# A two-layer trunk on one core: x of a token group asked for ahead of its weights, two small loads moved behind

## The chip, the cores and the metric

The kernel runs on one core of a Trainium2 chip. The metric is the device time of one execution in microseconds (us). The core has five engines with a queue of instructions each: PE (matrix products), DVE and POOL (elementwise), ACT (functions and copies) and SP, which here only issues transfers. An engine takes its instructions in the order of its queue; where one waits for a semaphore, all behind it wait too. Transfers between memory and the core run on 16 DMA engines.

## The reference, cut to what matters

The kernel computes a trunk of two layers for two batches with the same weights, 512 and 2048 tokens, width 1024:

```
def _even_layer(x, ...):
    p = _rmsnorm(x, norm_w) @ w_in                    # 1024 -> 4224 columns
    shifted = _centred_shift(p[..., :EVEN_SHIFT], mu_prev, mu_next)
    r, k, v, w_lat, a_lat = _split(shifted, ...)
    y_a = _rwkv7(...)                                 # w_up, a_up: rank 64 -> 512, two directions
    y_b = _dilated_attention(...)
    return x + concat(y_a * silu(gate_a), y_b * silu(gate_b)) @ w_out
def _odd_layer(x, ...):                               # gated linear attention, two directions
    ...
```

A final normalization by rows ends it. What this change touches is the first line (x is normalized and multiplied by `w_in`) and the loading of `w_up` and `a_up`, the up projections of the recurrent branch.

## The kernel before, in words

The 2560 tokens are worked in five groups of 512. For one group, `dense` multiplies the normalized, transposed x with blocks of 128 columns of the weights. All factors are split into a high and a low part, so that a block is 24 products of 128x128 by 128x512 (three for each of eight slices of the depth): `pd<-xh,wh`, `pd<-xl,wh`, `pd<-xh,wl` at L296.

`xprep` makes x ready: it loads four tiles of 128 tokens (L234), squares each on ACT (L237), finds the root of the mean on DVE (L239 and L205 to L210), scales the tiles by pairs on DVE (L242), transposes them on PE (`pt<-cst,x`, L248), multiplies by the norm's weights on ACT (L249) and splits them (L250, L251). The transposes of one slice take parts of all four tiles, so that the first block product needs all of x.

`weights` loads a block's weights in halves (`w`, L265, four buffers) and splits them into `wh` (L273) and `wl` (L274). `dense` creates it and takes the first two splits before it asks for x.

`open_prep` opens the buffers of the recurrent branch's preparation and loads at once the up projections (`PT<-in_wup`, L368, two loads of 512 KB), splits them (`wup`, cast on ACT L369, subtraction on DVE L370), and loads the pattern of the scan (`scan`, L372). The source of these two loads is 64 rows, broadcast to twice 64. They are read by `prep` (L455, L466), which runs beside the second group.

Further on, `inverts` inverts small triangular matrices for the recurrence: DVE makes `LD` (L580), PE multiplies (`pt<-LD,LO`, L589). `recurrence` then runs 80 steps (`pg`, `pc`), with attention beside it; out projections (`po`) and the second layer follow. `mix` and `weave` set how much of a side work is written between the steps of a main one, but the order of the instructions in the engines' queues is set by a scheduler when the program is built: it follows its own estimate of times, so that a small change at the start can move instructions anywhere behind it.

Of the kernel before, what the change touches and what calls it, by code (L numbers as in the profile page):

```python
# [117 lines left out]
class Trunk:  # L118
# [159 lines left out]
    def dense(self, parts, xT=None):  # L278

        nc = self.nc  # L280
        flat = [(p, n, *job) for p, (_, jobs) in enumerate(parts) for n, job in enumerate(jobs)]
        ws = self.weights(flat)
        split = [next(ws), next(ws)]
        xT = [] if xT is None else xT
        for p, n, _, m, sink in flat:
            if n == 0 and parts[p][0]:
                yield from parts[p][0](xT)
            ps = self.pd.tile([128, 512], F32, name="pd")
            byk = n == 0 or n == len(parts[p][1]) - 1
            for half in range(2):  # L290
                wh, wl = split.pop(0)
                split.extend(w for w in (next(ws, None),) if w)
                three = [((wh, k, hi), (wh, k, lo), (wl, k, hi)) for k, (hi, lo) in enumerate(xT[4 * half:4 * half + 4])]
                three = [e for t in three for e in t[:3 if byk else 2]] + [t[2] for t in three if not byk]
                for j, (a, k, x) in enumerate(three):
                    nc.tensor.matmul(ps[:m], a[:, k, :m], x, start=half == 0 and j == 0, stop=half == 1 and j == 11)  # L296
                    if j % 6 == 5:
                        yield 1280
            sink(ps)
# [62 lines left out]
    def open_prep(self, es):  # L362
        self.pq = self.pool(es, "pq", 1)
        self.ps_p = self.pool(es, "psp", 3, space=PSUM)
        self.wup = [self.pq.tile([128, 2, 512], F32R, name=f"wup{n}") for n in range(2)]
        for n, w in enumerate(self.wup):
            raw = self.pq.tile([128, 2048], F32, name="PT", bufs=2)[:, 0:1024].rearrange("p (z c) -> p z c", z=2)
            self.nc.sync.dma_start(raw, self.I["wup"][64 * n:64 * n + 64][None].to_broadcast([2, 64, 2, 512]))  # L368
            self.nc.scalar.copy(w, raw)  # L369
            self.nc.vector.tensor_tensor(w[64:128], raw[64:128], w[64:128].bitcast(F32), op=OP.subtract)  # L370
        self.scan = self.pq.tile([128, 520], F32, name="scan")
        self.nc.sync.dma_start(self.scan, self.I["scan"])  # L372
# [775 lines left out]
    def gla_unit(self, z, h, t0, first, S, tens, late):  # L1148
# [12 lines left out]
        for n in (0, 2):  # L1161
            duo = order[n:n + 2]
            At, kx = (gp.tile([128, 2, 128], F32, name=n, bufs=3) for n in ("at", "kx"))
            nc.gpsimd.memset(At[b, :, a], 0.0)
            pa = self.pa.tile([128, 2, 256], F32, name="pa")
            for i, s in enumerate(duo):
                kc = whole(K, s)
                kl = kc[:, 64:192] if z == 0 else kc[:, 0:128]
                nc.tensor.matmul(pa[:, i, b], kl, Q[:, s, 2 * se], start=True, stop=True)  # L1169
            for i, s in enumerate(duo):  # L1170
                nc.tensor.transpose(pa[:, i, 128:256], whole(KX, s), self.cc("ident"))
            for i, s in enumerate(duo):
                nc.tensor.matmul(pa[a, i, a], K[:, s, 2 * fi], Q[:, s, 2 * fi], start=True, stop=True)  # L1173
                within[s] = At[:, i], kx[:, i]
            nc.scalar.copy(kx, pa[:, :, 128:256])
            for c in (a, b):
                V.tensor_tensor(At[c, :, c], pa[c, :, c], m[c, None, :].to_broadcast([64, 2, 64]), op=OP.mult)
            nc.scalar.copy(At[a, :, b], pa[a, :, b])
            yield 860
        for s in order:  # L1180
            At, kx = within[s]
            po = self.pgo.tile([128, 2, 256], F32, name="pgo")
            qc = whole(Q, s)
            ql = qc[:, 0:128] if z == 0 else qc[:, 64:192]
            nc.tensor.matmul(po[:, 1], kx, Vt[:, s], start=True, stop=True)  # L1185
            nc.tensor.matmul(po[:, 0], At, Vt[:, s], start=True, stop=False)  # L1186
            nc.tensor.matmul(po[:, 0], ql, S, start=False, stop=True)  # L1187
            V.scalar_tensor_tensor(S, S, d[:, s, 2:3], po[:, 1], op0=OP.mult, op1=OP.add)
            if not late:
                nc.scalar.copy(o[:, s], po[:, 0])  # L1190
            else:
                V.tensor_tensor(o[:, s], po[:, 0], o[:, s], op=OP.add)
            yield 1300
# [67 lines left out]
    def whole(self):  # L1261
        I = self.I
        shifted, rest = [12] + list(range(12)), list(range(13, 33))
        left, right, base = ExitStack(), ExitStack(), ExitStack()

        def on(side, es):

            es.close()
            self.side = side
            return es  # L1270

        self.open_inv(on("right", base))
        self.open_prep(on("left", left))
        self.open_dense(on("right", right), 0)
        xT = []

        def part(t, blocks):

            xT.clear()
            return self.dense([(lambda x: self.xeven(x, t), self.even(t, blocks))], xT)  # L1280

        def behind(t):

            yield from self.inverts()
            yield from self.prep(1, t)

        self.run(part(0, shifted))
        self.mix(part(512, shifted), self.prep(0, 0), 0.6)
        for t in (1024, 1536, 2048):
            self.mix(part(t, shifted + rest), behind(t - 512), 0.72)  # L1290
        self.mix(part(0, rest), self.weave(self.inverts(), self.prep(1, 2048), 0.8), 1.0)
        self.open_dense(on("right", right), 2)
        xT.clear()
        self.run(self.xeven(xT, 512))
        self.xes.close()

        def beside():
            inv = self.inverts()
            for n in self.dense([(None, self.even(512, rest))], xT):
                yield n  # L1300
                next(inv, None)
            yield from inv
            right.close()
            base.close()
            for seq in range(2):
                self.open_att(on("right", right), seq)
                yield from self.attention(seq)

        self.open_rec(on("left", left))
        self.mix(self.recurrence(), beside(), 1.3)  # L1310
        self.open_out(on("right", right), 0, I["woe"])
        for t in (0, 1024, 1536, 512):
            self.run(self.out0(t))
        self.open_dense(on("left", left), 1)
        xT = []
        self.run(self.odd(1024)[0](xT), self.out0(2048))
        self.open_gla(on("right", right))
        until = lambda g, t: self.run(iter(lambda: next(g), t))
        g0, g1 = self.gla(0, PARTS[1:], (2048,), self.states()), self.gla(1, PARTS[:0:-1], (512, 1024, 1536), self.states())
        for t, now in ((1024, ()), (512, ((g0, 512), (g0, 1024))), (2048, ((g1, 2048),)), (1536, ((g0, 1536), (g1, 1536)))):  # L1320
            self.run(self.dense([(None, self.odd(t)[1])], xT) if t == 1024 else self.dense([self.odd(t)]))
            for g in now:
                until(*g)
        self.run(x for xs in zip(iter(lambda: next(g0), 2048), iter(lambda: next(g1), 1024)) for x in xs)
        self.run(self.dense([self.odd(0)]))
        self.run(g0)
        self.open_out(on("left", left), 1, I["woo"])
        self.fn = self.op.tile([128, 1024], F32, name="fn", bufs=1)
        f = I["fn"]
        self.nc.sync.dma_start(self.fn, bass.AP(tensor=f.tensor, offset=f.offset, ap=[[0, 128], [1, 1024]]))  # L1330
        S = self.states()
        p = chain(self.gla(0, [0], (), S), self.gla(1, [0], (0,), S))
        self.run(x for xs in zip(g1, p) for x in xs)
        self.run(g1, p, *(self.out1(t) for t in (1536, 2048, 1024, 512, 0)))
        right.close()
        left.close()
# [25 lines left out]
```

## Time and profile before

| what | value |
|---|---|
| median of 3 runs | 4209.18 us |
| the three runs | 4193.99, 4209.18, 4211.28 us |
| the profiled execution | 4192.46 us, its span 4190.7 us |
| PE busy | 3809.9 us (91% of the span) |
| DVE busy | 2624.2 us (63%) |
| ACT, POOL busy | 1790.0, 1465.4 us |
| mean granted clock of PE | 0.933 |

Busy times are sums over the span; what an engine's idle time costs depends on who waits for it there. A row of the order of time gives the start, the length, the engine, the line, and the tile written and read; in square brackets it says how long the engine stood idle before, and what ended that. "SPq" is the queue from which SP issues transfers.

### The profile page before, as it was taken

How to read it: one execution, taken by the hardware profiler on the slowest of the kernel's cores; microseconds unless marked ns; L12 is line 12 of the kernel's file. 1: busy time of each engine (PE TensorE's matmuls, PEld its weight loads, DVE VectorE, ACT ScalarE, POOL GpSimd, SP SyncE). 2: the span in 40 equal slices, each digit the busy share in tenths (PEclk: the TensorE clock that was granted, in tenths of full speed). 3: DMA queues.
4: the chain of work that ended last, by engine and by line, in shares of the span. 5: the costliest groups of instructions: out<-in, count | busy, mean ns of one | idle time of the engine just before them, and what ended most of it. 6: DMA issues, size and time to landing. Idle time of an engine off the chain costs nothing. (4 is left out here: it accounts for less than half of the span.)

```text
span 4190.7 us, 76827 instructions
## 1 busy us (share of the span) xinstructions
PE 3809.9 (91%) x28720; PEld 3001.9 (72%) x28720; DVE 2624.2 (63%) x6104; ACT 1790.0 (43%) x3685; POOL 1465.4 (35%) x1431
## 2 busy tenths in 40 slices
PE   5998988898787898999999997999999999988997
PEld 4776767677566776677777675778788787867776
DVE  4788887877978646456676755332354526576775
ACT  3453534443343234444544443112354526464552
POOL 2554635445554323112222322222343424232321
PEclk9999999999889888898998988999999999989999
DMA  5554645555445444534454435654554454555553
GB/s 161 186 190 141 191 139 180 163 174 166 149 149 165 131 126 139 161 110 148 127 157 120 138 85 175 207 176 138 161 166 155 156 159 156 180 191 171 172 177 126
DMA packets 516360, 655.78 MB, mean 156 GB/s; under 512 B 48083, under 2 KB 340179, under 8 KB 514963
## 3 DMA queue, kind: packets, MB, share of 16 engines
q1 hardware_dynamic: 422899, 562.72, 43.1%
q10 hardware_dynamic: 80464, 72.09, 5.4%
q0 software_dynamic: 12624, 16.06, 1.5%
q8 instruction: 227, 3.72, 0.4%
q14 instruction: 146, 1.20, 0.1%
HBM read 444.57 MB, written 206.36 MB: 155 GB/s over the span
## 5 line engine op out<-in xcount | busy, mean ns | idle before, releaser
L296 PE MATMUL pd<-xh,wh 128*128 128x512 f32 (+1 forms) x2320 | 944.2, 410 | 48.7 <-DVE wh L273 24.2
L296 PE MATMUL pd<-xl,wh 128*128 128x512 f32 (+1 forms) x2320 | 944.5, 407 | 20.3 <-POOL xl L251 19.7
L296 PE MATMUL pd<-xh,wl 128*128 128x512 f32 (+1 forms) x2320 | 690.4, 404 | 16.8 <-DVE wl L274 15.0
L274 POOL TENSOR_TENSOR wl<-w,wh 128x512 fp32r<-128x512 f32 (+1 forms) x290 | 396.3, 1367 | 670.6 <-PE pd L296 365.3
L296 PEld LDWEIGHTS pd<-xh,wh 128*128 128x128 f32 (+1 forms) x2320 | 447.1, 193 | 163.2 <-DVE wh L273 31.2
L296 PEld LDWEIGHTS pd<-xl,wh 128*128 128x128 f32 (+1 forms) x2320 | 448.3, 193 | 125.1 <-POOL xl L251 26.3
L296 PEld LDWEIGHTS pd<-xh,wl 128*128 128x128 f32 (+1 forms) x2320 | 439.7, 192 | 119.5 <-DVE wl L274 20.4
L273 DVE CAST wh<-w 128x512 fp32r<-128x512 f32 (+1 forms) x290 | 171.5, 591 | 346.6 <-PE pd L296 293.8
L273 ACT CAST wh<-w 128x512 fp32r<-128x512 f32 (+1 forms) x290 | 177.6, 613 | 327.8 <-PE pd L296 201.7
L896 ACT ACTIVATE P<-P,O 128x128 f32<-128x128 f32 (+2 forms) x480 | 198.1, 450 | 229.9 <-DVE O L894 222.6
L1031 PE MATMUL po<-oh,yh 128*128 128x512 f32 x640 | 257.4, 403 | 40.6 <-ACT yh L1020 40.6
L885 PE MATMUL pS<-Ks,Qs 64*128 64x256 f32 x896 | 274.2, 587 | 6.3 <-DVE O L894 4.1
L274 DVE TENSOR_TENSOR wl<-w,wh 128x512 fp32r<-128x512 f32 (+1 forms) x290 | 239.7, 827 | 62.8 <-PE pd L296 56.3
L1031 PE MATMUL po<-ol,yh 128*128 128x512 f32 x640 | 255.9, 401 | 0.0
L894 DVE CUSTOM_DVE_ANT_0 P<-pS,msk 128x128 f32<-128x128 f32 (+2 forms) x480 | 153.8, 353 | 156.9 <-PE pS L885 102.0
L1031 PE MATMUL po<-oh,yl 128*128 128x512 f32 x640 | 248.4, 400 | 2.6 <-DVE yl L1021 2.4
L934 PE MATMUL pV<-Vt,Pt 128*64 128x65 f32 (+1 forms) x3072 | 182.0, 246 | 20.4 <-DVE O L935 7.5
L934 PEld LDWEIGHTS pV<-Vt,Pt 128*64 128x64 f32 (+1 forms) x3072 | 136.8, 148 | 78.0 <-issue 23.6
L723 POOL TENSOR_TENSOR X<-X,wcs 64x512 f32<-64x512 f32 x76 | 80.1, 1054 | 319.5 <-PE pc L761 181.5
L885 PEld LDWEIGHTS pS<-Ks,Qs 64*128 64x128 f32 x896 | 150.3, 270 | 54.6 <-issue 16.8
L1018 POOL TENSOR_TENSOR yr<-yr,yg 128x1024 f32<-128x1024 f32 x40 | 97.8, 2446 | 257.3 <-DMA yr<-d_yT 170.9
L546 POOL TENSOR_TENSOR PTr<-PTr,wc 128x512 f32<-128x512 f32 x80 | 84.9, 1061 | 285.4 <-PE pg L536 261.0
(285 smaller groups left out, 7612.2 us busy)
## 6 DMA issues: line engine op xcount, KB each, us to landing
w<-in_we SPq DMA_DIRECT2D x330, 256.0 KB
w<-in_wi SPq DMA_DIRECT2D x240, 256.0 KB
d_f<-PT SPq DMA_DIRECT2D x40, 1024.0 KB
PTr<-d_f SPq DMA_DIRECT2D x77, 512.0 KB
d_sg<-st SPq DMA_DIRECT2D x80, 256.0 KB
yr<-d_yT SPq DMA_DIRECT2D x40, 512.0 KB
yg<-d_sg SPq DMA_DIRECT2D x40, 512.0 KB
Vg<-d_gv SPq DMA_DIRECT2D x40, 512.0 KB
```

The source lines that it names most:

```text
L273: (nc.vector.tensor_copy, nc.scalar.copy)[h](wh[:, :, :m], w[:, :, :m])
L274: (nc.vector, nc.gpsimd)[h].tensor_tensor(wl[:, :, :m], w[:, :, :m], wh[:, :, :m].bitcast(F32), op=OP.subtract)
L296: nc.tensor.matmul(ps[:m], a[:, k, :m], x, start=half == 0 and j == 0, stop=half == 1 and j == 11)
L546: nc.gpsimd.tensor_tensor(bk, bk, self.wc[:, z, c, :, None].to_broadcast([128, 4, 128]), op=OP.mult)
L723: nc.gpsimd.tensor_tensor(nx, x[lo, 0], self.wcs[:, z, c, :, None].to_broadcast([64, 8, 64]), op=OP.mult)
L885: nc.tensor.matmul(o2, a[o], b[o], start=True, stop=True)
L894: V.tensor_tensor_reduce(P[:, h, :nk], pss[h][:, u, off:off + nk], mask, 1.0, 3e38, op0=OP.add, op1=OP.min, accum_out=m)
L896: nc.scalar.activation(P[:, h, :nk], P[:, h, :nk], AF.Exp, scale=-1.0, bias=m)
L934: nc.tensor.matmul(po[q, h, :], Pt[:r, i, h, q], v[:r, h, :], start=i == 0, stop=i == n - 1)
L1018: nc.gpsimd.tensor_tensor(y, y, g, op=OP.mult)
L1031: nc.tensor.matmul(ps[u][e], a[:, k], b[:, k, c], start=k == 0 and j == 0, stop=k == 7 and j == 2)
```

## The change

Two edits. In `dense`, the first two steps of the first part's `xprep` (which issue the loads of x, square and scale it) are now written before `weights` is created, and the rest of it where all of it stood. In `open_prep`, only the buffers are opened; the loads of the up projections and of the scan's pattern are in a function of its own, `load_prep`, which is called after 14 steps of the first group's `dense` (two steps of x, eight slices, one block of four steps).

```
         flat = [(p, n, *job) for p, (_, jobs) in enumerate(parts) for n, job in enumerate(jobs)]
+        xT = [] if xT is None else xT
+        fill = parts[0][0](xT) if parts[0][0] else iter(())
+        for _ in range(2):
+            yield from (n for n in (next(fill, None),) if n)
         ws = self.weights(flat)
         split = [next(ws), next(ws)]
-        xT = [] if xT is None else xT
         for p, n, _, m, sink in flat:
-            if n == 0 and parts[p][0]:
-                yield from parts[p][0](xT)
+            if n == 0:
+                yield from parts[p][0](xT) if p else fill
...
     def open_prep(self, es):
         self.pq = self.pool(es, "pq", 1)
         self.ps_p = self.pool(es, "psp", 3, space=PSUM)
+
+    def load_prep(self):
         self.wup = [self.pq.tile([128, 2, 512], F32R, name=f"wup{n}") for n in range(2)]
...
-        self.run(part(0, shifted))
+        first = part(0, shifted)
+        for _ in range(14):
+            next(first)
+        self.load_prep()
+        self.run(first)
```

What the scheduler makes of it. The queue of SP at the start of the program, before (`w` are weights, `x` the tokens, `PT<-in_wup` the up projections):

```order
L154 DMA cst<-in_cst 128x579
L157 DMA par<-in_par 128x88
L368 DMA PT<-in_wup 128x1x1024 x2
L372 DMA scan<-in_scan 128x520
L265 DMA w<-in_we 128x512 x4
L234 DMA x<-in_xp 128x1024 x4
L356 DMA rope<-in_rope 128x2x512
L265 DMA w<-in_we 128x512 x3
```

The same place now:

```order
L154 DMA cst<-in_cst 128x579
L157 DMA par<-in_par 128x88
L234 DMA x<-in_xp 128x1024 x4
L265 DMA w<-in_we 128x512 x4
L373 DMA PT<-in_wup 128x1x1024 x2
L377 DMA scan<-in_scan 128x520
L359 DMA rope<-in_rope 128x2x512
L265 DMA w<-in_we 128x512 x3
```

x and the first four weight tiles went to the front, the up projections and the scan's pattern behind them.

The queue of ACT at the start, as a piece of the difference (+ is now; `wup` are the up projections, `xr<-pt` is the first step on the transposed x):

```order
-L369 CAST wup_110<-PT 128x1024
-L369 CAST wup_111<-PT 128x1024
-L273 CAST wh<-w 128x512
+L1367 UNCONDITIONAL_BRANCH
+L237 ACT_TABLE_LOAD
 L237 ACTIVATE xr,ss<-x 128x1024 x4
+L273 CAST wh<-w 128x512
+L374 CAST wup_330<-PT 128x1024
+L374 CAST wup_331<-PT 128x1024
 L249 ACTIVATE xr<-pt,par 128x512 x2
```

The casts of the up projections moved behind the four squares of x, and stand ahead of L249. On DVE, before, the two subtractions of `wup` stand ahead of all of x's steps; now they stand between the scaling of the first pair of x and that of the second:

```order
L242 TENSOR_SCALAR x<-x,xry 128x1024 x2
L205 TENSOR_SCALAR xri<-ms 128x2
L273 CAST wh<-w 128x512
L206 TENSOR_SCALAR xry<-xri 128x2
L274 TENSOR_TENSOR wl<-w,wh 128x512
L208 SCALAR_TENSOR_TENSOR xru<-xry 128x2
L209 TENSOR_TENSOR xru<-xru,ms 128x2
L210 SCALAR_TENSOR_TENSOR xry<-xru,xry 128x2
L208 SCALAR_TENSOR_TENSOR xru<-xry 128x2
L209 TENSOR_TENSOR xru<-xru,ms 128x2
L375 TENSOR_TENSOR wup_330<-PT,wup_330 64x1024
L210 SCALAR_TENSOR_TENSOR xry<-xru,xry 128x2
```

The second subtraction follows two rows later, and after two more small steps the scaling of the second pair (L242). So both stand ahead of it.

Further on, on PE, where the last inversions are multiplied (`pt<-LD,LO`) between the block products of a group and the first steps of the recurrence, before:

```order
L296 MATMUL pd<-xh_12278,wl 128x512
L296 MATMUL pd<-xh_12280,wl 128x512
L296 MATMUL pd<-xh_12282,wl 128x512
L296 MATMUL pd<-xh_12284,wl 128x512
L536 MATMUL pg<-PTr 128x128 x8
L747 MATMUL pc<-X,BK 64x64 x8
L550 MATMUL pc<-cst,PTr 128x128 x2
L589 MATMUL pt<-LD,LO 32x32 x64
```

And now:

```order
L299 MATMUL pd<-xh_12276,wh 128x512
L299 MATMUL pd<-xl_12277,wh 128x512
L299 MATMUL pd<-xh_12270,wl 128x512
L299 MATMUL pd<-xh_12272,wl 128x512
L299 MATMUL pd<-xh_12274,wl 128x512
L299 MATMUL pd<-xh_12276,wl 128x512
L541 MATMUL pg<-PTr 128x128 x2
L594 MATMUL pt<-LD,LO 32x32 x64
L762 MATMUL pc<-X,RS 64x64 x8
```

Counted by the block products (`pd`) that stand ahead of it in the program, this multiplication moved back by 60, and the one after it by 42.

## Rows read from the trace of the kernel before

**Rows 1.** The page: span, and busy us (share) by engine.

```profile
span 4190.7 us, 76827 instructions
PE 3809.9 (91%) x28720; PEld 3001.9 (72%) x28720; DVE 2624.2 (63%) x6104; ACT 1790.0 (43%) x3685; POOL 1465.4 (35%) x1431
```

**Rows 2.** Busy time of each engine in stretches of the span.

```profile
core 0: us, PE busy (x) PEld busy (x) DVE busy (x) ACT busy (x) POOL busy (x), PEclk, DMA share, GB/s
0.00:47.00 47.00, 4.29 (x16) 2.75 (x17) 13.21 (x41) 10.35 (x15) 3.10 (x15) 1.00 0.44 136
47.00:140.00 93.00, 91.28 (x429) 74.58 (x428) 52.69 (x92) 42.16 (x71) 43.96 (x42) 1.00 0.50 162
...
1060.00:1400.00 340.00, 274.04 (x2153) 215.78 (x2149) 297.14 (x452) 126.22 (x244) 173.12 (x162) 0.88 0.47 144
1400.00:2500.00 1100.00, 1038.00 (x12691) 775.60 (x12691) 643.67 (x2329) 514.47 (x1318) 267.85 (x283) 0.90 0.46 134
```

**Rows 3.** PE's waits, whole span: for whom, total us, times, longest us.

```profile
PE pt L248 <- DVE x L242: 42.1, 2, 39.7
```

**Rows 4.** The start in order of time, SP's queue: start us, us.

```profile
1.21 0.42 SPq L157 DMA_DIRECT2D par<-in_par  x1
1.66 1.32 SPq L368 DMA_DIRECT2D PT<-in_wup  x2
3.03 9.85 SPq L372 DMA_DIRECT2D scan<-in_scan  x1
12.92 4.67 SPq L265 DMA_DIRECT2D w<-in_we  x4
17.64 12.87 SPq L234 DMA_DIRECT2D x<-in_xp  x4
```

**Rows 5.** The start in order of time, DVE, ACT and PE.

```profile
3.72 0.17 DVE L162 TENSOR_SCALAR c<-par 128x13 f32<-128x13 f32 x1 [3.72 <-DMA par<-in_par]
...
17.31 1.04 ACT L369 CAST wup<-PT 128x1024 fp32r<-128x1024 f32 x1 [15.27 <-DMA PT<-in_wup]
...
29.53 1.04 ACT L369 CAST wup<-PT 128x1024 fp32r<-128x1024 f32 x1 [11.17 <-DMA PT<-in_wup]
30.60 1.22 DVE L370 TENSOR_TENSOR wup<-PT,wup 64x1024 fp32r<-64x1024 f32 x1 [10.99 <-ACT wup L369]
...
34.08 1.06 ACT L237 ACTIVATE xr<-x 128x1024 bf16<-128x1024 f32 x1 [1.97 <-DMA x<-in_xp]
...
40.26 0.16 DVE L239 TENSOR_SCALAR ms<-ss 128x2 f32<-128x2 f32 x1
...
42.62 1.42 DVE L242 TENSOR_SCALAR x<-x,xry 128x1024 f32<-128x1024 f32 x2
...
47.03 1.20 PE L296 MATMUL pd<-xh,wh 128*128 128x512 f32 x2
...
54.36 0.97 DVE L273 CAST wh<-w 128x512 fp32r<-128x512 f32 x1 [0.69 <-PE pd L296]
```

**Rows 6.** DMA queues from 7 to 13 us: packets, MB, share of 16 engines.

```profile
DMA packets 79, 0.32 MB, mean 53 GB/s; under 512 B 2, under 2 KB 2, under 8 KB 79
...
q1 hardware_dynamic: 77, 0.32, 12.8%
```

**Rows 7.** Busy times from 32 to 36 us, columns as in rows 2.

```profile
32.00:36.00 4.00, 0.00 (x0) 0.00 (x0) 3.00 (x4) 1.89 (x4) 1.26 (x1) 1.00 0.92 342
```

**Rows 8.** Who reads wup: durations ns, first and last start us.

```profile
L455 PEld LDWEIGHTS pp<-lat0h,wup x40: 186/190/331, 130.2 to 1272.7; 128*128 128x128 f32 x40
```

**Rows 9.** PE's waits from 1060 to 1400 us.

```profile
PE pt L589 <- DVE LD L580: 10.2, 2, 6.9
```

**Rows 10.** PE in order of time near 1400 us.

```profile
1394.04 3.83 PE L589 MATMUL pt<-LD,LO 32*32 32x32 f32 x128 [6.91 <-DVE LD L580]
...
1403.35 0.40 PE L296 MATMUL pd<-xh,wh 128*128 128x512 f32 x1
1403.59 0.40 PE L296 MATMUL pd<-xl,wh 128*128 128x512 f32 x1
```

## The prediction, made before the changed kernel ran

> **What bounds the kernel now.** I read the page's busy times first: the matrix engine (PE) works 3809.9 us of a 4190.7 us span, DVE 2624.2 [rows 1]. So time can only be won where PE stands idle, 381 us in all. The table of stretches shows where: 42.7 us before 47 us, then 1.7 us of the 93 to 140, 66 us of the 340 between 1060 and 1400 (there DVE is busy 297), 62 us of the 1100 after it [rows 2]. The table of PE's waits names the ends: 42.1 us in two waits for the scaled x (DVE, L242), one of them 39.7 us long [rows 3]. That is the very start. Everything else that ends on x is 2.4 us. So of the edit in `dense`, which holds for every token group, only the first group has a wait to give back. The order says the same: of the later groups the x loads stand behind the same number of weight loads as before, but for one tile of the 512 group (two weight loads later).
>
> Then I read the start in order of time. SP asks for cst, par, the two up-projection loads (PT<-in_wup), scan, four weight tiles, and only then x; the issue of scan is held for 9.85 us, that of x for 12.87 us [rows 4]. ACT gets the first up-projection tile at 17.31, the second at 29.53, the first x at 34.08; the second x pair is scaled from 42.62, and the first block product starts at 47.03 [rows 5]. Why so late, with 16 DMA engines? From 7 to 13 us only the up-projection loads move: 77 packets, 0.32 MB, 12.8% of 16 engines, so two engines at 26 GB/s each [rows 6]. Later, with x and w in the queue, 342 GB/s pass [rows 7].
>
> The Trainium skill ("DMA: Bandwidth & Descriptors", section "Why a DMA increments its semaphore by 16 and not by 1") has the rule: a transfer is spread over the largest number of engines up to 16 that divides the slowest dimension, always the lowest-numbered ones; the up-projection's source begins with a dimension of 2 (the broadcast), so 2 engines, the same two for both loads. The trace agrees with the same two: were they two pairs, rows 6 would have to read 25%. By the other reading the second load would land some 10 us sooner and the gain below would be 13 us in place of 3.
>
> **The change, part by part.**
>
> *x and w in front on SP.* x (4 x 512 KB) and w (4 x 256 KB) now stand ahead of the two up-projection loads. par, issued at 1.21, is used at 3.72 [rows 4, 5], so data follow an issue by about 2.5 us, and x, issued from about 1.7, moves from about 4.2. One sixteenth of x is 131 kB, at 26 GB/s 5.0 us: x has landed by some 11 us, against 34.
>
> *But the two up-projection loads still stand in front of the first block product.* The order on ACT and DVE (shown in the section on the change) decides: ACT has both casts of wup ahead of the first activation on the transposed x (L249), and DVE has both subtractions ahead of the scaling of the second x pair (L242). An engine's instructions go in order, so x waits for the second up-projection load after all. That load now stands behind x and w on its two engines: one sixteenth of 3.15 MB is 197 kB, 7.5 us at 26 GB/s, 9.2 us at 342 GB/s over all engines. It was cast at 29.53; I add 7.5: 37.0. From there: the cast until the subtraction, 30.60 - 29.53 = 1.07; the subtraction 1.22; two small steps, 0.4; from the start of L242 to the first block product 47.03 - 42.62 = 4.41 [rows 5]. Sum 37.0 + 7.1 = 44.1 us. **Start: -2.9 us.** Bounds: if the two engines lose nothing on the way (2 x 512 KB over two engines at 26 GB/s is 20.2 us, from 4.2 + 7.5), the load is there at 31.9 and the start gains 8; by 9.2 us it gains 1.2; if each of the two loads begins moving only 2.5 us after the one before has ended, it loses 3.8. I take 2.9, since it rests on the landing that was seen.
>
> *Weights of the third block, scan and rope.* They now stand behind the up-projection on those two engines: 260, 512 and 256 KB, a sixteenth each, is 2.5 us after about 37, so about 40 to 42. The third block's first weight tile was cast at 54.36 [rows 5]; the cover is some 10 us, cost nothing. wup is first read by prep at 130.2 [rows 8], the scan's pattern in the step after: nothing. The rest of the edit (two steps of x ahead of the weight casts) adds no instruction.
>
> *The order further on.* The scheduler lays the whole program out again. Up to about 850 us, and from 2500 to 3700, PE's order is nearly the same; between, blocks of it move. The largest move with a wait behind it: the last inversion's products (pt<-LD) come 60 and 42 block products later. Before, PE stood 6.91 us at 1394.04 until DVE had LD [rows 10]. DVE has LD at nearly the same place of its own order, so the block products now fill that wait. After it PE is busy 1038 of 1100 us [rows 2], so what it did early it needn't do late. Ends: a gain of 10.2 us (both waits for LD in that stretch [rows 9], one of 6.9 and one of 3.3), a loss of 14 (below). I take the row itself: **-6.9 us.**
>
> Sum: -2.9 - 6.9 = -9.8 us. Against the profiled execution, 4192.46 us (span 4190.7), that is 4182.7; the median of the three runs, 4209.18, lies 16.7 above it, and on that scale the forecast is 4199.4 us.
>
> **Rivals.**
>
> *A. x reaches PE without the up-projection.* If wup's casts did not hold ACT and DVE, the last x at about 11 would be followed by one square (1.06), the twelve small DVE steps (42.62 - 40.26 = 2.36) and the 4.41 to the first product [rows 5]: 19; with the weights' casts in between some 20, a gain of 27; with the 6.9 above, 4175. For it: x does land that early. Against it: the order of two engines.
>
> *B. Slower: the recurrence gets its inverse later.* Place: 1394 us, where the last inversions end. They stand 60 block products later on PE, at 0.235 us a product (the starts in [rows 10]) 14.1 us. The recurrence reads these inverses through memory. If the recurrence, and not PE, bounds the stretch to 2500, the 14.1 us are lost and the 6.9 not won: 4209.2 - 2.9 + 14.1 = 4220.4. It decides as soon as the recurrence waits for its inverse. For it: 1060 to 1400 is bound by DVE (297 of 340). Against it: PE is 94% busy behind it.
>
> *C. The change does not do what it says.* The start stays at 47 us or later (bound +3.8), the order moves nothing net: 4206 to 4213.
>
> **How the numbers follow.** Forecast 0.50, A 0.06, B 0.16, C 0.28. The three runs of before lie 17 us apart, as much as all cases but A differ; a change of under 0.5% (21 us) can't be told from none here. Faster than that is below 4188: A nearly whole (0.05), and from the forecast and C what the scatter gives (0.19): 0.24. Slower is above 4230: a third of B and a little of C, 0.07. The rest, 0.69, is no change. The range reaches from A's upper part to B's time: 4174 to 4220; the forecast's own is 4186 to 4211.
>
> **What would show it.** In the profile after: x loads issued from about 1.7 us; the first x square at 7 to 9 us, not 34; the second cast of wup at about 37 (32 to 39), ACT idle before it and waiting for that DMA; the first block product at about 44. If that product starts before 30, A is right; at 47 or later, C. Near 1390 no wait of PE for LD of several us: the forecast; a wait of the recurrence for its inverse or PE idle between 1400 and 1500: B. The sum is wrong if some other stretch between 850 and 2500 moves by more than 10 us.

## The result

The changed kernel is slower: 4220.32 us (median of 10 runs, 4204.77 to 4243.18), beside 4209.09 us for the kernel before in the same comparison (10 runs, 4193.40 to 4214.63); ratio over all runs 1.0052, interval 1.0035 to 1.0069. (The quotient of the medians is smaller, 1.0027: four of the ten runs of the kernel before lie at 4193 to 4195 us, six at 4209 to 4215.) The forecast was 4199. In the profiled executions it is 4232.33 us against 4192.46: the changed kernel's is the eighth of its ten by time, that of the kernel before is below all ten of its own, so the 40 us between these two are about twice the difference of the kernels. Lines behind L281 have moved by three to five in the file: L299 is the former L296, L353 the former L350, L585 and L594 the former L580 and L589.

### The start went as forecast

SP's queue and the engines in order of time, in the profile of the changed kernel (start us, length us; columns as in [rows 4, 5], to which these rows answer):

```profile
1.67 2.02 SPq L234 DMA_DIRECT2D x<-in_xp  x4
3.73 2.98 SPq L265 DMA_DIRECT2D w<-in_we  x4
8.63 2.90 SPq L373 DMA_DIRECT2D PT<-in_wup  x2
11.57 9.87 SPq L377 DMA_DIRECT2D scan<-in_scan  x1
...
26.49 1.04 ACT L374 CAST wup<-PT 128x1024 fp32r<-128x1024 f32 x1 [12.19 <-DMA PT<-in_wup]
...
37.24 1.04 ACT L374 CAST wup<-PT 128x1024 fp32r<-128x1024 f32 x1 [9.71 <-DMA PT<-in_wup]
38.31 1.22 DVE L375 TENSOR_TENSOR wup<-PT,wup 64x1024 fp32r<-64x1024 f32 x1 [9.14 <-ACT wup L374]
...
39.96 1.42 DVE L242 TENSOR_SCALAR x<-x,xry 128x1024 f32<-128x1024 f32 x2
40.77 1.35 PE L248 MATMUL pt<-cst,x 128*128 128x128 f32 x4 [23.44 <-DVE x L242]
...
44.35 1.20 PE L299 MATMUL pd<-xh,wh 128*128 128x512 f32 x2
```

Read it from the bottom: the first block product waits for the scaled x, x on DVE stands behind the subtraction of wup, this behind ACT's cast at 37.24, and the cast waits 9.71 us for the second up-projection load. The first block product is at 44.35, before at 47.03 [rows 5].

### The loss is further on, and most of it is PE working at a slower clock

The page's first lines of the changed kernel, beside [rows 1]:

```profile
span 4230.5 us, 76830 instructions
PE 3842.8 (91%) x28720; PEld 3028.5 (72%) x28720; DVE 2623.4 (62%) x6104; ACT 1790.0 (42%) x3685; POOL 1461.9 (35%) x1431
```

The same 28720 products keep PE busy 32.9 us longer (3842.8 - 3809.9); the span grew by 39.8. So 33 of the 40 us are not waiting: the products themselves took longer. A part of that is the choice of these two executions, but not all: three profiled executions with the order of before (the kernel before, its repeat and its version with the split load below) have PE busy for 3810 to 3827 us, four with the changed order for 3837 to 3845. DVE and ACT are as busy as before. What can make the same product longer here is the granted clock, so the next view has to be the table of stretches with its PEclk column. To compare the two kernels the stretches are cut where PE has the same work behind it (each shape of product counted with the time between starts that it has in the trace of before). First the kernel before, then the changed one (us, busy us and count of PE, PEld, DVE, ACT, POOL, granted clock, DMA share, GB/s):

```profile
47.00:140.00 93.00, 91.28 (x429) 74.58 (x428) 52.69 (x92) 42.16 (x71) 43.96 (x42) 1.00 0.50 162
140.00:1264.00 1124.00, 992.68 (x7029) 789.87 (x7028) 933.32 (x1436) 486.87 (x913) 588.42 (x568) 0.93 0.53 167
1264.00:1500.00 236.00, 201.63 (x1985) 159.24 (x1983) 153.49 (x241) 76.89 (x159) 95.69 (x88) 0.90 0.49 148
1500.00:1900.00 400.00, 372.56 (x4372) 275.13 (x4370) 225.52 (x855) 185.39 (x489) 89.72 (x99) 0.85 0.47 134
1900.00:2560.00 660.00, 616.25 (x7697) 458.69 (x7696) 424.09 (x1567) 319.46 (x818) 166.66 (x175) 0.90 0.44 127
2560.00:4190.00 1630.00, 1531.26 (x7200) 1241.67 (x7200) 821.87 (x1877) 668.89 (x1221) 477.86 (x447) 0.97 0.53 168
```

```profile
44.00:142.00 98.00, 93.69 (x429) 76.38 (x428) 50.86 (x91) 41.89 (x71) 42.74 (x42) 0.98 0.46 153
142.00:1265.00 1123.00, 994.89 (x7033) 791.68 (x7032) 926.63 (x1424) 487.79 (x914) 589.40 (x568) 0.93 0.53 167
1265.00:1511.00 246.00, 203.89 (x1979) 162.01 (x1977) 161.54 (x252) 77.38 (x159) 94.94 (x88) 0.85 0.46 142
1511.00:1926.00 415.00, 380.26 (x4386) 282.18 (x4386) 226.91 (x859) 183.76 (x488) 89.73 (x98) 0.84 0.45 130
1926.00:2603.00 677.00, 631.28 (x7696) 468.07 (x7690) 423.38 (x1564) 321.00 (x819) 165.97 (x175) 0.88 0.43 124
2603.00:4230.00 1627.00, 1534.79 (x7200) 1245.76 (x7200) 821.44 (x1877) 667.91 (x1221) 475.92 (x448) 0.97 0.52 168
```

Up to 1264 us both are equal but for 5 us behind the start; behind 2560 they are equal too. Between, the changed kernel takes 1338 us for what took 1296: 10 more, 15 more, 17 more. The clock is lower in each of the three rows. But they are not alike: of the first row's 10 us, 8 are PE standing idle (34.4 us before, 42.1 now); of the 32 us of the other two, 23 are PE's busy time.

Most of the 5 us are seen at 84 us. DVE and PE in order of time, changed kernel:

```profile
82.27 1.42 DVE L242 TENSOR_SCALAR x<-x,xry 128x1024 f32<-128x1024 f32 x2
83.72 0.42 DVE L421 CAST lat0l<-lat0l 64x512 fp32r<-64x512 f32 x1
84.17 0.43 DVE L273 CAST wh<-w 128x512 fp32r<-128x512 f32 x1
84.66 0.50 PE L299 MATMUL pd<-xh,wh 128*128 128x512 f32 x1 [3.08 <-DVE wh L273]
84.99 0.46 PE L299 MATMUL pd<-xl,wh 128*128 128x512 f32 x1
85.25 0.63 PE L299 MATMUL pd<-xh,wh 128*128 128x512 f32 x1
```

The scaling of the next group's x now stands ahead of a weight cast on DVE; PE waits 3.08 us (0.8 before, the longest wait for wh in that stretch), and right behind it the same product goes from 0.46 to 0.63 us: the clock has dropped to its half level for a few us.

PE's waits from 1265 to 1511 us, changed kernel (for whom, total us, times, longest us), where [rows 9] showed 10.2 us of waiting for LD:

```profile
PE pd L299 <- DVE st L353: 11.2, 2, 7.4
PE pg L541 <- issue: 8.6, 2, 4.5
PE pd L299 <- DVE tmp L329: 5.4, 2, 4.0
PE pd L299 <- ACT xh L250: 5.4, 1, 5.4
PE pt L594 <- issue: 4.1, 1, 4.1
```

LD is gone from the top, as forecast; other waits stand in its place. And the inversions, that now come later, come all at once. PE in order of time near 1420 us, changed kernel, then the stretch around it:

```profile
1414.55 0.80 PE L299 MATMUL pd<-xh,wh 128*128 128x512 f32 x1 [3.97 <-DVE tmp L329]
...
1420.64 3.80 PE L594 MATMUL pt<-LD,LO 32*32 32x32 f32 x128 [0.23 <-DVE LD L585]
1424.37 1.12 PE L762 MATMUL pc<-X,RS 64*64 64x64 f32 x16
...
1426.67 3.46 PE L602 MATMUL pt<-XT,N 32*32 32x32 f32 x122
...
1437.41 1.83 PE L594 MATMUL pt<-LD,LO 32*32 32x32 f32 x57 [4.10 <-issue]
```

```profile
1419.00:1443.00 24.00, 19.67 (x468) 17.66 (x467) 11.03 (x12) 6.92 (x15) 8.41 (x8) 0.57 0.39 119
```

For 24 us PE does only small products, no block product among them, at a granted clock of 0.57; the 16 products `pc<-X,RS` take 1.12 us here, and 0.68 in the kernel before at 1406.98, at the full clock. Before, the last two inversions started 14 us apart (the first at 1394.04 [rows 10]), with 18 block products between them. The clock is low there too, in the kernel before:

```profile
1386.00:1404.00 18.00, 11.09 (x167) 9.45 (x164) 14.33 (x20) 3.51 (x6) 7.11 (x8) 0.62 0.27 74
1404.00:1420.00 16.00, 15.34 (x327) 12.98 (x326) 6.62 (x6) 6.68 (x13) 3.93 (x4) 0.79 0.42 142
```

Against the full clock that is 10.2 us (0.38 of 18 and 0.21 of 16), and 10.3 in the changed kernel (0.43 of 24). So it is not the slow clock at the inversions themselves that parts the two kernels; the changed one's lower mean in this row (0.85 against 0.90) comes from other places in it.

### The profile page after: what moved, and what is told of

It reads as the page before. It is cut to its first block, busy times and chain, and to the rows that moved or that the text cites. A ratio compares the mean times of both kernels' runs of the same rounds, so it can differ in the third digit from the quotient of the medians.

```text
span 4230.5 us, 76830 instructions
## 1 busy us (share of the span) xinstructions
PE 3842.8 (91%) x28720; PEld 3028.5 (72%) x28720; DVE 2623.4 (62%) x6104; ACT 1790.0 (42%) x3685; POOL 1461.9 (35%) x1431
## 5 line engine op out<-in xcount | busy, mean ns | idle before, releaser
L299 PE MATMUL pd<-xh,wh 128*128 128x512 f32 (+1 forms) x2320 | 948.6, 412 | 66.9 <-DVE wh L273 25.0
L299 PE MATMUL pd<-xl,wh 128*128 128x512 f32 (+1 forms) x2320 | 947.0, 408 | 15.7 <-POOL xl L251 15.6
L299 PE MATMUL pd<-xh,wl 128*128 128x512 f32 (+1 forms) x2320 | 689.3, 404 | 22.2 <-DVE wl L274 18.7
L299 PEld LDWEIGHTS pd<-xh,wh 128*128 128x128 f32 (+1 forms) x2320 | 449.1, 194 | 180.8 <-DVE wh L273 31.3
L299 PEld LDWEIGHTS pd<-xl,wh 128*128 128x128 f32 (+1 forms) x2320 | 450.4, 194 | 120.2 <-POOL xl L251 21.1
L299 PEld LDWEIGHTS pd<-xh,wl 128*128 128x128 f32 (+1 forms) x2320 | 439.8, 192 | 127.0 <-DVE wl L274 25.6
```

## The experiments

The kernels of one comparison ran on the same chip beside runs of the kernel before; ratios are to those.

### The result again, and the parts alone

No edit in the first; then only the edit of `dense`; only that of `load_prep`; both, with `load_prep` after 2 steps in place of 14; and the kernel before with its loads put into `load_prep` but called at once, which leaves its order as it was:

```
-        for _ in range(14):
+        for _ in range(2):     # both, at step 2;  range(0) without the edit of dense: the kernel before
```

> The changed kernel once more, to have a second trace of it. The theory (the start gives 2.7 us, the moved order behind it takes them back and more) expects a time around 4220 us, and that the same stretches lose again: about 4 us between 75 and 90 us, where a weight's cast on DVE comes late, and 10 to 20 us between 1264 and 1450 us, around the last inversions. The rival (the first trace of it was an unlucky one, the loss lies in the recurrence's granted clock alone) expects the losses before 1450 us to be gone or elsewhere.

Measured: 1.0053 (1.0034 to 1.0071), first block product at 42.72. The loss is the kernel's and repeats; the stretch from 1256 to 1501 us, the one of 246 above, takes 245 again.

> Only the edit in dense: x of a group is asked for ahead of its weights; the up projections are loaded at the very start as before. On SP their loads stand in front of x again. The start should be within 1 us of before (47 us): no gain. Its order puts the last inversions 24 and 32 block products earlier than before did, and is the changed kernel's own from the recurrence on. If the loss comes from the late inversions, this kernel is within 5 us of before; if it comes from the order in the recurrence and attention, it is 10 to 20 us slower than before, as the changed one is.

Measured: 1.0007 (0.9994 to 1.0019), first block product at 47.66: alone, x in front of w gives nothing at the start. By its own test this is within 5 us and not 10 to 20 slower, although it has the changed kernel's order in the recurrence; the section on the late order comes back to it.

> Only the second edit: the up projections and the scan's pattern loaded behind the first blocks, the weights still ahead of x. Its start should be that of the changed kernel within 1 us (first block product at 44 to 45 us): the two-engine loads still stand in front of the activation on the transposed x. It has the last inversions 74 and 56 block products later than before. If late inversions cost, it is the slowest of these, 20 us over before or more; if not, within 5 us of before.

Measured: 0.9989 (0.9973 to 1.0004), first product at 44.73. In this kernel the last inversions stand later still than in the changed one (3800 block products ahead of the last one's second half in the order, against 3780; before 3738), and it is the fastest of the parts. So late inversions do not by themselves hold up the recurrence.

> Both edits, with the up projections asked for after 2 steps in place of 14: x, then the up projections, then the weights on SP. Start at 41 to 44 us. From the recurrence on its order is that of before; the last inversions stand as late as in the changed kernel (60 and 42 block products). If late inversions cost, it loses 10 to 20 us there and ends 8 to 17 us over before; if the order in the recurrence and attention costs, it is 0 to 5 us faster than before.

Measured: 1.0011 (0.9997 to 1.0025), first product at 45.12. Both edits, the early start, another order: the loss is all but gone. The two theories of this run are not parted by it: 1.0011 is some 5 us over before, between their ranges.

> The kernel before, written with the new function but calling it at once, so that every engine's order is that of before: a second trace of the old order. It should time within 0.1% of before. Theory (the changed order is slower because TensorE stands at half its clock for more of the time, not because it waits more): in this trace the time at half clock over the whole span is within some 40 us of before's 556, where the two traces of the changed kernel have 640 or so, and PE's idle time in the recurrence is the same in all. Rival (before's first trace was a lucky one, both orders are equal): it has 600 us or more at half clock.

Measured: 0.9999 (0.9981 to 1.0016): the function of its own costs nothing. Its profile has a mean granted clock of 0.930 over 4205.8 us; with the two levels of full and half that is some 590 us at the half clock, within the theory's 40 of 556, if barely, and against 643 by the same sum for the changed kernel (0.924 of 4230.5).

### Taking the up-projection load off the path

The source of this load begins with a broadcast of 2, and rows 6 showed two engines busy. Two loads of 64 rows each write the same tile:

```
-            self.nc.sync.dma_start(raw, self.I["wup"][64*n:64*n+64][None].to_broadcast([2,64,2,512]))
+            for h in range(2):
+                self.nc.sync.dma_start(raw[64*h:64*h+64], self.I["wup"][64*n:64*n+64])
```

It leaves the order of each kernel as it was. First the kernel before with it:

> The kernel before, with each up-projection load issued as two loads of 64 rows in place of one broadcast, so that it can spread over all DMA engines; every engine's order is otherwise that of before. Up projections, scan's pattern, weights and x are 4.46 MB, at 342 GB/s from 4.2 us moved by 17.2; with 2 us for landing and 8 us from the last x to the first block product, that product starts at 27 us in place of 47: 19 us less in all, some 4185 to 4190 (0.4 to 0.5% faster). If the two engines are not what holds the start, it stays at 47 us and the time is unchanged.

Measured: 0.9949 (0.9927 to 0.9972), 4182.86 us beside 4204.39, the first product at 28.81. The start of that kernel, stretches and order of time:

```profile
4.00:8.00 4.00, 0.00 (x0) 0.00 (x0) 0.46 (x6) 0.00 (x0) 0.00 (x0) 1.00 1.04 238
8.00:13.00 5.00, 0.00 (x0) 0.00 (x0) 1.55 (x2) 3.37 (x3) 0.00 (x0) 1.00 1.04 295
```

```profile
10.37 2.18 ACT L370 CAST wup<-PT 128x1024 fp32r<-128x1024 f32 x2
...
15.88 1.06 ACT L237 ACTIVATE xr<-x 128x1024 bf16<-128x1024 f32 x1 [2.01 <-DMA x<-in_xp]
...
28.81 1.20 PE L296 MATMUL pd<-xh,wh 128*128 128x512 f32 x2
```

All 16 engines are busy (share 1.04, against 0.128 in [rows 6]), both casts of wup are done at 12.55 (10.37 + 2.18), where the second one began at 29.53 before [rows 5], x is squared from 15.88 and not from 34.08. The shape of these two loads held x, and with it the first block product, for 18 us. This is the rule of the Trainium skill ("DMA: Bandwidth & Descriptors", section "Why a DMA increments its semaphore by 16 and not by 1") that the forecast had read for these two loads; here the trace bears it out. Then the changed kernel with the same edit, and the one at step 2:

> The changed kernel with the same split of the two loads, orders otherwise those of the changed kernel. x lands as it did (first square at 8.6 us), the second up projection at 18 to 19 us in place of 37, so the first block product starts at 25 to 26 us in place of 44: 18 us less than the changed kernel, some 4204, about the time of before. The theory that the changed order costs 25 us behind the start says that it stays 15 to 22 us slower than before_spread's 4185, though both start within 3 us of each other. The rival that the order does not matter says that it equals it or is 2 us faster.

> Both edits with the up projections asked for after 2 steps (r4's order) and the loads split. First block product at 24 to 26 us. Against r4, whose start was at 45 us, 18 us less: some 4190 to 4193. If the order of r4 is worth as much as that of before, it ends within 5 us of the kernel before with split loads.

Measured: 1.0023 (1.0005 to 1.0042), 4213.82 us, first product at 29.58; and 0.9976 (0.9956 to 0.9997), first product at 30.54. The kernel before and the changed one, each with the split, start within 0.8 us of each other and end 31 us apart, where 15 to 22 were expected. What costs is the order behind the start. The order of step 2 is not worth as much as that of before either: it ends 14 us behind the kernel before with the split, where at most 5 were expected.

### The wait at 1335 us

Of the new waits the longest, 7.4 us for st, comes from ACT: its queue issues the recurrence's first loads and stands 14.60 us, and the activation that st needs is behind them:

```profile
1333.51 0.82 ACT L548 COPY RS<-PTr 64x256 f32<-64x256 f32 x2 [14.60 <-DMA X<-d_v]
```

Issued from SP:

```
-            load(s, nc.scalar)
-            state(s, nc.scalar)
+            load(s)
+            state(s)
```

> The changed kernel, with one thing else: the recurrence's first three pairs of loads (PTr and X) are issued by SP and no longer by ACT, whose queue is held for 14.6 us at 1319 by these issues, so that the silu's tanh comes late and PE waits 7.36 us at 1335. Theory 1 (the lost time of 1264 to 1500 comes from the activations that stand behind these issues): the 7.4 us wait falls below 3 us, this stretch takes about 240 us in place of 246.6 and 245.6, the whole is some 6 us faster than the changed kernel, 4214 beside 4209 of the kernel before (ratio 1.001 to 1.003). Theory 2 (the order brings so much time at the half clock there, 72 us against 45 to 49, whatever the waits): the wait goes, but the stretch stays at 244 us or more and the ratio at 1.004 to 1.006. The first block product stays at 43 to 45 us by both.

Measured: 1.0085 (1.0064 to 1.0106). The wait fell to 3.5 us, and the stretch from 1260 to 1505 still takes 245 us. Theory 1 fell: the wait was halved and none of its time was won. The ratio lies above the range of theory 2 as well, and why is not shown. PE's waits in that stretch (1240 to 1500 us), with the loads on SP:

```profile
PE pg L541 <- issue: 7.7, 2, 6.2
...
PE pd L299 <- DVE st L353: 3.5, 1, 3.5
```

> The kernel before with the up-projection's load split in two of 64 rows (4183 when it ran beside 4209), and the recurrence's first loads issued by SP. In the kernel before ACT is held 10.5 us at 1304 by these issues, and PE then waits 2.5 and 2.0 us for st. Theory 1: both waits go, some 4 us: 4179 (ratio 0.993 to 0.995). Theory 2 (the wait moves to the next late thing, or the loads now stand behind weight loads on SP and the recurrence starts later): 4183 to 4190. First block product at 28.5 to 30.

Measured: 0.9970 (0.9953 to 0.9986), no better than with the split alone. This edit is not a clean test: by the trace, PE's order between some 1310 and 1870 us is another one too, with the last two inversions next to each other.

> The edit of load_prep alone (4197 when it ran beside 4209) with the split load. The scheduler makes of it an order of its own, unlike all others run so far. If the start were all, it would take 16 us less than the same edit with the unsplit load, 4181 (ratio 0.993 to 0.995), with the first block product at 29. If each order has its own price of up to 30 us, which no count of moved blocks tells beforehand, it may lie anywhere from 4180 to 4212 with the same first product.

Measured: 0.9971 (0.9950 to 0.9993), 4182.11 us beside 4194.00, first product at 29.77. The start came 17 us earlier than that of the kernel before, and 12 of them are left at the end: the start is not all.

### Giving each kernel the other's late order

One number sets at what share the last inversions are woven with the last projections, and by it the scheduler's late order can be turned without touching the start:

```
-        self.mix(part(0, rest), self.weave(self.inverts(), self.prep(1, 2048), 0.8), 1.0)
+        self.mix(part(0, rest), self.weave(self.inverts(), self.prep(1, 2048), 0.9), 1.0)   # changed kernel
+        ... 0.6 and 0.7 in the kernel before
```

The changed kernel with 0.9 has, instruction for instruction, PE's order of the kernel before from block product 3467 on (but for a piece of 20 of them) up to the last stage; the kernel before with 0.6 has that of the changed one from block product 3468 on; with 0.7 it keeps, by the order of the starts in its trace, that of the kernel before up to 1787 us (but for short pieces) and has that of the changed one from there on. (The expectation below puts this at some 1500 us.)

> The changed kernel with one number of the scheduler's changed: the share at which the last inversions are woven with the last projections is 0.9 in place of 0.8. Up to the third tenth of the program it stands in the order of the changed kernel (x in front, the weight casts late at 84 us), from some 1400 us on exactly in that of the kernel before: the last two inversions stand 19 block products apart and no longer behind each other. Theory 1 (the order from 1264 to 2560 costs the 25 to 30 us, by time at the half clock): that stretch takes what it took in the kernel before (236 us for 1264 to 1500, granted clock 0.90 and not 0.85), the mean granted clock is 0.930 to 0.932 and not 0.924, and the whole lies at -2.7 at the start and +4 at 84 us, some 0 to 5 us faster than the kernel before (ratio 0.998 to 1.001). Theory 2 (the price comes from what stands before, the earlier start itself or the order up to 1264 us): ratio 1.004 to 1.007 as the changed kernel's. First block product at 43 to 45 us by both.

Measured: 0.9975 (0.9954 to 0.9995), 4190.23 us beside 4203.46. The changed start with the late order of before is faster than before. Its stretches:

```profile
1258.00:1497.00 239.00, 200.88 (x1987) 158.35 (x1985) 154.14 (x235) 76.48 (x158) 95.69 (x88) 0.89 0.48 145
1497.00:1897.00 400.00, 372.76 (x4372) 275.08 (x4370) 227.02 (x859) 185.42 (x490) 89.96 (x99) 0.85 0.47 134
1897.00:2563.00 666.00, 620.77 (x7698) 462.05 (x7696) 423.58 (x1567) 318.78 (x818) 166.73 (x175) 0.89 0.43 126
```

236, 400 and 660 before; 246, 415 and 677 in the changed kernel; 239, 400 and 666 here. And the wait for LD, whose end was the forecast's gain, is in this faster kernel longer than in the kernel before (6.91 [rows 10]):

```profile
1388.79 3.83 PE L594 MATMUL pt<-LD,LO 32*32 32x32 f32 x128 [10.42 <-DVE LD L585]
```

> The converse of the run with 0.9: the kernel before, its start and loads untouched, with the weaving share at 0.6 in place of 0.8. Up to block product 3296 (about 1240 us) PE has the order of the kernel before, from product 3468 on exactly that of the changed kernel. Theory 1 (the late order is the whole price): slower than the kernel before by 20 to 30 us, 1264 to 1500 at a granted clock of 0.85 to 0.87, mean clock 0.924 to 0.926, ratio 1.004 to 1.007, first block product at 47. Theory 2 (the late order costs only together with the changed kernel's early part, as when an early lead sets the phase of what follows): ratio 0.998 to 1.002.

Measured: 1.0071 (1.0047 to 1.0095), 4233.86 us beside 4201.76. The late order alone makes the kernel before slow, though its start and loads are untouched. (Its profiled execution is by 20 us the fastest of its six, so its stretches are not shown.)

> The kernel before with the share at 0.7: its order to some 1500 us with the last two inversions 19 products apart as before, and from there (PE instruction 8102 of 20078 in the order) exactly the changed kernel's order. It parts the late order in two. If the loss lies where the inversions and the recurrence's start meet, from 1264 to 1500: that stretch as before (235 us, 0.90), ratio 0.999 to 1.002. If most lies in the order of the recurrence from 1500 to 2560: ratio 1.003 to 1.006, that stretch 1080 to 1100 us in place of 1060.

Measured: 1.0044 (1.0028 to 1.0060), 4217.51 us. Its stretches:

```profile
1270.00:1502.00 232.00, 197.68 (x1984) 156.05 (x1982) 152.80 (x240) 76.39 (x159) 95.13 (x87) 0.90 0.50 148
1502.00:1922.00 420.00, 390.47 (x4372) 288.03 (x4372) 224.80 (x857) 185.99 (x489) 89.65 (x98) 0.81 0.46 128
1922.00:2589.00 667.00, 622.64 (x7696) 461.04 (x7696) 424.38 (x1566) 320.36 (x819) 166.03 (x175) 0.90 0.44 126
```

1264 to 1500 is as fast as before (232 us at 0.90), and what follows takes 1087 us in place of 1060. So the late order costs some 18 us (0.0044 of 4202) even where the last inversions stand as before. The 11 us or so by which the kernel with 0.6 is slower still (1.0071) would be the price of the place where the last inversions meet the recurrence's first steps; but the two intervals overlap, so this second price is not shown by the times.

Where do the 18 us lie? Between 1500 and 2560 us this kernel's order differs from that of the kernel before in two places of more than 40 products, at 1787 to 1873 and at 2177 to 2361 us of the kernel before; both are products of the recurrence (`pg`, `pc`) woven with those of attention. The first place at the same 1012 products, before and then with 0.7:

```profile
1787.00:1873.00 86.00, 84.74 (x1012) 62.40 (x1006) 42.89 (x161) 40.98 (x106) 13.77 (x15) 0.92 0.38 109
1793.00:1895.00 102.00, 102.00 (x1012) 74.38 (x1009) 41.80 (x162) 41.57 (x107) 13.71 (x15) 0.77 0.34 92
```

PE never stands idle in the slower one; the same products take 16 us more at a lower clock. The 17 profiled kernels sort by the order of this piece: seven with that of before took 82 to 90 us for it, seven with that of the changed one 91 to 103, three with an order of their own 88 to 90. At the second place it is 179 to 187 us against 187 to 196. This sorts traces; no run turned one of the two pieces alone.

One kernel speaks against a fixed price. The edit of `dense` alone has, from some 1470 us on, the order of this kernel on PE, DVE, ACT and POOL, but for a few records, and its profile has the slow piece too (102.6 us). Yet it lost 0.0007 (at most 0.0019), where this one lost 0.0044. Its order differs mostly between 900 and 1470 us; whether that wins back what the late order costs is not shown, since its one profiled execution is the slowest of its 13 runs.

> The changed kernel with the share at 0.9 (4190 beside 4203) and the up-projection's load split in two of 64 rows. By both theories the gains add: 13 us from the order, some 14 to 16 more from the start (first block product at 29.6): 4174 to 4177 where the kernel before takes 4203, ratio 0.993 to 0.995. If the split kernel before (0.995) already has all that can be had, it is not below 0.995.

Measured: 0.9958 (0.9936 to 0.9980), 4186.75 us, first product at 29.17. It beats the kernel before, but not the kernel before with the split load (0.9949): the two can't be told apart, and of the 13 us that the same kernel with the unsplit load had against the kernel before, nothing is seen on top of the start's gain.

The mean granted clock, median over the runs of each kernel, sorts those with either late order by that alone, whatever their start; those with a part of it or an order of their own lie between or with the kernel before:

| late order | kernels: mean granted clock |
|---|---|
| that of before | before 0.930 to 0.932; before again 0.9295; before, split 0.931; changed with 0.9 0.932; the same, split 0.9305 |
| that of changed | changed again 0.924; changed, split 0.924; changed, loads on SP 0.9245; before with 0.6 0.9235 |
| that of changed in its later part only | before with 0.7 0.928; `dense` alone 0.927 |
| others | step 2 0.927, split 0.9285; `load_prep` alone 0.931, split 0.932; before, split, loads on SP 0.933 |

0.007 of 4200 us is 29 us: the size of the loss. It is a rough measure: by it `dense` alone and step 2, 0.004 below the kernel before beside them (0.931), would lose some 17 us, and they lose 3 and 5 by their ratios.

## Why the prediction was wrong

*Start, -2.9.* Right. The cast of the second wup tile came at 37.24 (forecast 37.0), the first block product 2.7 us earlier. The reading behind it, that the two up-projection loads on their two engines hold x through the order of ACT and DVE, is borne out by the split: without it the first block product comes 18 us earlier in the kernel before and 15 in the changed one.

*Third block, scan and rope at nothing, x ahead of the weight casts at nothing.* Right for the first group. For the second it missed: x of the next group now stands in front of a weight cast on DVE at 84 us, some 5 us (98 in place of 93 for that stretch, half of them PE idle, the rest PE busy longer). It is not the edit of `dense` by itself: `load_prep` alone has the same order there and a wait of 2.2 us as well. The prediction had counted of the later groups only their loads, not their steps on DVE.

*The order further on, -6.9.* This is the step that failed. It named one wait, found that it would go, and it went. It took for granted that the rest of the order between 850 and 2500 us would cost the same, because PE was 94% busy there. But 94% busy is not a fixed amount of work: the same 28720 products took 32.9 us more of PE's time, at a lower granted clock. In place of -6.9 the late order costs about 30 (the kernel before with 0.6: 1.0071, with its interval 20 to 40 us), and the kernel that keeps the wait for LD, at 10.42 us, is the faster one. The prediction's own alarm, another stretch moving by over 10 us, went off.

*Rival B.* It had the sign, and its 4220.4 is the measured median, but not the mechanism: it wanted the recurrence to wait for its inverses. They stand latest in the kernel with `load_prep` alone, which loses nothing; and the kernel with 0.7 loses 18 us with its inverses where they were. The agreement of the number is chance.

*Rival A* fell as argued, by the order of ACT and DVE. *C* was right only in that the start gave little.

What stays open is why one order of the same products gets a lower clock than another. For 1264 to 1500 the last two inversions are a likely mark: where they stand together without block products between, the stretch took 238 to 247 us in nine profiled kernels; where block products stand between or within them, 229 to 239 in eight. The ranges touch, and it is a grouping of traces, not an experiment of its own. Behind 1500 the waits add up to 71 us before and 80 in the changed kernel, and the remaining 23 us of the 32 are PE's busy time; the two pieces of recurrence and attention above hold 22 of the 27 us by which the kernel with 0.7 is longer there, but in the profile of the changed kernel itself only 9 of its 32, and `dense` alone, with both pieces, is hardly slower. One kernel's runs also differ among themselves by as much as the kernels do: the kernel before ran at 0.927 to 0.938, 4175 to 4207 us, in 23 runs of one comparison.

## What to carry to other kernels

When a scheduler lays out the whole program again, a few us at the start buy a new order for all that follows; here that order cost up to some 30 us, ten times what the edit won at the start. Compare PE's busy time at an equal count of products and the granted clock by stretches before crediting a wait that goes. And look at a transfer's share of the DMA engines before moving it: giving the load a shape that all 16 can work on won 21 us in the kernel before, where moving it behind x brought the first block product forward by 3.

## What the runs showed of the hardware

A load of 512 KB whose source begins with a dimension of 2 kept a queue of transfers at 53 GB/s [rows 6]; the same bytes in two loads of 64 rows moved at 238 to 295 GB/s together with their neighbours. The granted clock depends on the order of the same instructions in a repeatable way (0.924 against 0.931 over 6 to 35 runs each, on several chips), while single runs scatter by more than that difference. The same 1012 small products of recurrence and attention took 86 us at 0.92 in one order and 102 us at 0.77 in another, with PE idle for 1.3 us in the first and never in the second.
